# SSD convolutions in a queue of their own, and the last pair of an end stage leaving PSUM tile by tile

## The chip, the cores and the metric

The kernel runs on one core of one Trainium2 chip, in one launch. The metric is the device time of that core in microseconds. A core has five engines with a queue of instructions each: TensorE (PE in the profile, its weight loads PEld), VectorE (DVE), ScalarE (ACT), GpSimd (POOL) and SyncE (SP, which here issues most DMAs). Each works through its own queue in order, and waits at an instruction until what that needs from another engine is there.

## The reference

One step of a decoder layer for a prompt of 512 tokens and 8 sample requests of 4 tokens, which share the weights. All is fp32, D_MODEL is 1024.

```python
def layer(x, pos, rg_h0, rg_buf, ssd_h0, ssd_buf, p):
    x = x + 0.5 * rmsnorm(swiglu(rmsnorm(x, p['n_ffn1_pre']), p['ffn1_wg'], p['ffn1_wu'], p['ffn1_wd']), p['n_ffn1_post'])
    mix, new = mixer(rmsnorm(x, p['n_mix_pre']), pos, rg_h0, rg_buf, ssd_h0, ssd_buf, p)
    x = x + rmsnorm(mix, p['n_mix_post'])
    x = x + 0.5 * rmsnorm(swiglu(rmsnorm(x, p['n_ffn2_pre']), p['ffn2_wg'], p['ffn2_wu'], p['ffn2_wd']), p['n_ffn2_post'])
    return x, new
```

The mixer projects to one wide vector and works on two branches. The RG-LRU branch is a causal convolution over four tokens, two gates, a linear recurrence and a projection. The SSD branch is what the change touches:

```python
    xbc_c, ssd_buf_new = causal_conv(xbc, ssd_buf, p['ssd_conv_w'], p['ssd_conv_b'])
    xbc_c = jax.nn.silu(xbc_c.astype(f32))
    xs, Bs, Cs = jnp.split(xbc_c, [SSD_INNER, SSD_INNER + SSD_GROUPS * SSD_STATE], axis=-1)
    ...
    y, ssd_h_new = ssd_scan(xh, dt, A, Bs.reshape(b, l, SSD_GROUPS, SSD_STATE), Cs.reshape(b, l, SSD_GROUPS, SSD_STATE), ssd_h0)
    y = (y + p['ssd_d'][:, None] * xh).reshape(b, l, SSD_INNER) * jax.nn.silu(z.astype(f32))
```

There are 8 groups of 4 heads, with a state of 128 and chunks of 128 tokens; then come a grouped RMSNorm, a projection, a gated sum of the branches and an output projection. The last three inputs of each convolution are an output too (`ssd_buf_new`).

## The kernel before, in words

**Layout.** Prompt and samples are worked on together: 544 columns, in two halves of 272, with channels on the partitions. A matrix product is three products of rounded parts (high by high, low by high, high by low), so a block of 1024 by 128 weights takes 8 × 3 × 2 = 48 matmuls of 128x272. Such a block is a unit (`unit`, whose matmuls are L285): it fills one of two PSUM tiles named acc, of two banks each. `pair` takes one half of the columns and two blocks (L317 through `gemm_half`): bank j of acc is then tile j of the output. Weights come in blocks of 1 MB on SP's queue into wraw; ACT rounds a block to wh (L75) and DVE takes the rest as wl (L79), some blocks ahead of TensorE.

**Order.** TensorE's instructions run as they are written. The other engines' are put in order by a scheduler that goes by priorities; `urgent()` raises the priority of what stands under it. Small work for TensorE is woven between the matmuls of the units: `bg` is a list of generators, and after every `pace` matmuls (4 in the mixer, 5 after group 7's units) `ptick` calls `tick`, which runs the generator at the head up to its next `yield`. A generator starts when the one in front is through.

**The mixer.** After the RG-LRU pairs (`rg_steps`, four, of two tiles of 128 channels each) come eight SSD groups. For group g the units make four inputs of convolutions (B, C, and two tiles of x), then in some groups gates, then two tiles of z. For each of the four inputs ACT evacuates acc into a buffer cb (`conv_in`: L734 for the first half, L736 and L737 for the second) and copies the last three inputs of the prompt and of each sample to a small tile cq (`conv_last`, L877). Then a generator `conv_steps` is put behind in `bg`: it does the convolution (one ACT operation, L863, and three on DVE, L865), a tanh on ACT (L1009) and two products on DVE (L1010, L1011). In the second and the fourth of them, `conv_state` (from L879) first turns two cq tiles on TensorE (L884), copies them out on DVE (L887) and stores them. Behind these four, `bg` gets `group_steps`, which does the scan: A(c) for chunk c turns x and B into token order (L1041, L1043), evacuates them with DVE (L1056) and ACT (L1059) and makes the decays (L1048, L1062); Bs(c) makes the chunk's output (L1082, L1084) and state (L1086); s0, s1, s2 (L1165 with the evacuation L1168), s3 and s4 are for the samples; `fin` and the lines behind it finish the group. All tiles named ps share two PSUM buffers.

**End stages.** The last stage of FFN1, the output projection and FFN2 go through `y_units`, with halves and pairs. After a pair `evac_y` (L439 on DVE where the tile is added to what is there, or a copy on ACT), a square (L426), and a sum of squares (L433) follow. For the last pair (n2 == last) these are done tile by tile, but all of them after both tiles' matmuls. In FFN2's last pair, the final scaling yw (L1470) and turns to token order (L1474) follow at once.

## Time and profile before

| | |
|---|---|
| median of 3 runs | 1745.37 us (1741.66 to 1747.27) |
| the profiled execution's own time | 1746.04 us |
| its span, first to last instruction | 1744.2 us |
| TensorE busy | 1692.1 us, 97% |
| VectorE busy | 1000.7 us, 57% |
| ScalarE busy | 739.6 us, 42% |
| GpSimd busy | 260.4 us, 15% |
| mean granted clock of TensorE | 0.985 |

Times in the profile are microseconds from the start of the span. "L285" is line 285 of the kernel before. A row such as "PE ps L1041 <- ACT big L1168: 8.0, 5, 2.2" says that TensorE's instructions of line 1041 waited five times for ACT's of line 1168, for 8.0 us in all and 2.2 at most. In rows in order of time the first two numbers are start and length, and the bracket at the end gives the idle time of the engine just before, and who ended it. A PE row with x2 stands for two matmuls.

Groups 0 to 7 of the SSD branch lie between about 660 and 1075 us, FFN1 before 440 us, the output projection around 1240 to 1340 us and FFN2 behind it.

### The profile page before, as it was taken

The page shows a single profiled execution, that of the slowest core. Times are in us where ns is not written, and L with a number is a line of the kernel's source. Part 1 is how long each engine was busy: PE and PEld are TensorE (multiplying, and loading weights), DVE is VectorE, ACT ScalarE, POOL GpSimd, SP SyncE. Part 2 cuts the span into 40 slices and gives each one's busy share as a digit, 9 for nine tenths or more (in the row PEclk, how much of TensorE's full clock was granted, in tenths as well). Part 3 has the DMA queues.
Part 4 walks back from the last instruction along what each step waited for, and adds up shares of the span by engine and source line. Part 5 has one row for each costly group of instructions (what it writes and reads, how often), then busy time and mean ns, then how long its engine had stood idle before and what let it go on. Part 6 is the DMA issues. An engine that isn't in the chain of part 4 may idle for free. (4 is left out here: it accounts for less than half of the span.)

```text
span 1744.2 us, 32098 instructions
## 1 busy us (share of the span) xinstructions
PE 1692.1 (97%) x13485; PEld 1649.7 (95%) x13485; DVE 1000.7 (57%) x1764; ACT 739.6 (42%) x1204; POOL 260.4 (15%) x376
## 2 busy tenths in 40 slices
PE   8999999999999998999999999999999999999997
PEld 8899999999999997998988988999999999999997
DVE  5632333237757578788689687776558332233335
ACT  6323221234568674545545545434246423221233
POOL 0000000000222125345344333230000000000000
PEclk9999999999999998999999999999999999999999
DMA  6223232233543333524443535666324323223231
GB/s 208 84 75 114 74 98 84 87 97 109 164 156 112 101 97 107 165 88 113 146 144 93 157 114 155 214 189 221 137 80 139 115 68 109 85 85 97 75 120 52
DMA packets 205551, 206.21 MB, mean 118 GB/s; under 512 B 10461, under 2 KB 191785, under 8 KB 205150
## 3 DMA queue, kind: packets, MB, share of 16 engines
q1 hardware_dynamic: 196588, 178.49, 33.1%
q0 software_dynamic: 8336, 24.54, 4.3%
q8 instruction: 106, 1.74, 0.4%
q10 hardware_dynamic: 482, 1.12, 0.2%
q14 instruction: 39, 0.32, 0.1%
HBM read 178.43 MB, written 25.69 MB: 117 GB/s over the span
## 5 line engine op out<-in xcount | busy, mean ns | idle before, releaser
L75 ACT CAST wh<-wraw 128x1024 fp32r<-128x1024 f32 (+1 forms) x274 | 283.6, 1037 | 645.9 <-PE acc L285 535.0
L285 PE MATMUL acc<-xh,wh 128*128 128x272 f32 x2576 | 544.3, 292 | 0.1
L285 PE MATMUL acc<-xh,wl 128*128 128x272 f32 x2576 | 541.7, 292 | 0.0
L285 PE MATMUL acc<-xl,wh 128*128 128x272 f32 x2576 | 539.3, 291 | 0.0
L79 DVE TENSOR_TENSOR wl<-wraw,wh 128x1024 fp32r<-128x1024 f32 (+1 forms) x274 | 331.3, 1212 | 320.3 <-ACT wh L75 317.2
L285 PEld LDWEIGHTS acc<-xh,wh 128*128 128x128 f32 x2576 | 409.0, 190 | 3.5 <-issue 1.4
L285 PEld LDWEIGHTS acc<-xh,wl 128*128 128x128 f32 x2576 | 407.3, 190 | 2.6 <-issue 1.2
L285 PEld LDWEIGHTS acc<-xl,wh 128*128 128x128 f32 x2576 | 408.3, 190 | 1.2 <-issue 0.4
L317 PE MATMUL acc<-xh,wh 128*128 128x272 f32 x384 | 114.6, 298 | 3.3 <-DVE xl L571 3.3
L317 PE MATMUL acc<-xh,wl 128*128 128x272 f32 x384 | 113.8, 296 | 0.0
L317 PE MATMUL acc<-xl,wh 128*128 128x272 f32 x384 | 113.4, 295 | 0.0
L386 DVE TENSOR_TENSOR gate<-gate,acc 128x544 f32<-128x544 f32 x36 | 26.0, 721 | 132.0 <-PE acc L285 132.0
L865 DVE SCALAR_TENSOR_TENSOR cv<-cb,hp,cv 128x568 f32<-128x568 f32 x96 | 93.9, 978 | 1.1
L285 PE MATMUL acc<-hh,wh 128*128 128x272 f32 x448 | 92.5, 288 | 0.0
L285 PE MATMUL acc<-hl,wh 128*128 128x272 f32 x448 | 92.2, 287 | 0.0
L285 PE MATMUL acc<-hh,wl 128*128 128x272 f32 x448 | 92.2, 288 | 0.0
L1551 POOL TENSOR_TENSOR xtok<-xtok,yo 32x512 f32<-32x512 f32 x1 | 1.3, 1257 | 535.7 <-ACT yo L1550 535.7
L725 POOL MEMSET cb<- 128x3 f32 x40 | 4.1, 102 | 510.1 <-PE acc L317 434.7
L317 PEld LDWEIGHTS acc<-xh,wh 128*128 128x128 f32 x384 | 74.4, 194 | 3.9 <-DVE xl L571 3.4
L317 PE MATMUL acc<-hh,wh 128*128 128x272 f32 x256 | 75.0, 293 | 0.0
L317 PEld LDWEIGHTS acc<-xl,wh 128*128 128x128 f32 x384 | 74.4, 194 | 0.5
L317 PEld LDWEIGHTS acc<-xh,wl 128*128 128x128 f32 x384 | 74.2, 193 | 0.3
(397 smaller groups left out, 2642.5 us busy)
## 6 DMA issues: line engine op xcount, KB each, us to landing
wraw<-in_w_in_dram SPq DMA_DIRECT2D x34, 1024.0 KB, 5.6
wraw<-in_ffn_wu_dram SPq DMA_DIRECT2D x24, 1024.0 KB, 5.3
wraw<-in_ffn_wg_dram SPq DMA_DIRECT2D x23, 1024.0 KB, 5.2
wraw<-in_ffn_wd_dram SPq DMA_DIRECT2D x20, 1024.0 KB, 5.2
wraw<-in_w_in_dram SPq DMA_DIRECT2D x18, 512.0 KB, 4.3
big<-acs_dram SPq DMA_DIRECT2D x32, 256.0 KB, 5.6
big<-in_state_ssd_dram SPq DMA_DIRECT2D x32, 256.0 KB, 6.0
out_dram<-big POOLq DMA_DIRECT2D x32, 256.0 KB, 3.6
```

The costliest lines, as they stand in the source:

```text
L75: c = nc.scalar.copy(h[:, :kt], src)
L79: nc.vector.tensor_sub(l[:, :kt], src, h[:, :kt].bitcast(F32))
L285: PE.matmul(acc[:, h, :TH], w[:, k, :], r[k][:, HALF[h]], start=(k == 0 and i == 0), stop=(k == kt - 1 and i == 2))
L317: PE.matmul(acc[:, j, :TH], w[:, k, :], r[k][:, HALF[h]], start=(k == 0 and i == 0), stop=(k == kt - 1 and i == 2))
L386: V.tensor_mul(two(gs[j]), two(gs[j]), acc[:, :, :TH])
L725: G.memset(buf[:, 0:3], 0.0)
L865: V.scalar_tensor_tensor(o[:, :CO], buf[:, k:k + CO], ws[k], o[:, :CO], op0=ALU.mult, op1=ALU.add)
L1551: G.tensor_add(x[:n, cs], x[:n, cs], o[:n])
```

## The change

**First**, the four convolutions of a group are no longer generators in `bg`. They are plain functions (`conv_ssd`) in a list `convs`. `conv_next(g, limit)` takes the first of them if it is one of group g's, if fewer than `limit` of that group's have been taken, and if at least APART = 7 ticks have passed since the last. It is called at every `yield` of the group in front (`steps` in `group_steps`): the limit is 2 up to A(3), 3 up to s3(0) and Bs(2), 4 from there. The last RG-LRU pair takes up to two of group 0's. When `bg` is empty, `tick` takes one. What is left when a group starts is done at its start.

**Second**, `pair` takes a function `done(acc, j)`, called in program order after each tile's 24 matmuls. `y_units` gives it the evacuation for the last pair, so tile 0's evacuation, square, sum and (in FFN2) scaling are written ahead of tile 1's matmuls. Other pairs are as before.

```diff
+APART = 7
@@
+    def conv_take():
+        g, work = convs.pop(0)
+        work()
+        convs_done[g] += 1
+        conv_at[0] = ticks[0]
+
+    def conv_next(g, limit):
+
+        if convs and convs[0][0] == g and convs_done[g] < limit and ticks[0] >= conv_at[0] + APART:
+            conv_take()
+
     def tick():
+        ticks[0] += 1
         while bg:
...
+        if convs:
+            conv_next(convs[0][0], 4)
@@ pair
             gemm_half(acc, j, wbs[j], kt, rh, rl, h)
+            if done is not None:
+                done(acc, j)
@@ y_units
-            acc = pair(kt, rh, rl, h, keep if n2 in KEPT else None, n2)
...
-            step = 1 if n2 == last else 2
...
-            for j in range(0, 2, step):
+
+            def out(acc, j, step=1):
                 yv = yb[:, 2 * n2 + j:2 * n2 + j + step, HALF[h]]
                 with urgent():
                     evac_y(yv, acc[:, j:j + step, :TH], add)
...
+            acc = pair(kt, rh, rl, h, keep if n2 in KEPT else None, n2, out if n2 == last else None)
+            if n2 != last:
+                out(acc, 0, 2)
@@ rg_steps
+        def steps(n):
+            for _ in range(n):
+                yield
+                if r0 == KD - 2:
+                    conv_next(0, 2)
@@ conv_steps, now conv_ssd
-    def conv_steps(f, buf, res, i):
+    def conv_ssd(f, buf, res, i):
...
-        yield from wait(3)
@@ group_steps
+        while convs_done[g] < 4:
+            conv_take()
+            yield from wait(3)
         Bt, Ct, x0, x1, z0, z1 = (tiles[i] for i in range(6))
+        limit = [2]
+
+        def steps(n):
+            for _ in range(n):
+                yield
+                conv_next(g + 1, limit[0])
...
         A(3)
-        yield from wait(3)
+        limit[0] = 3
+        yield from steps(3)
         yield from s3(0)
         Bs(2)
-        yield from wait(3)
+        limit[0] = 4
+        yield from steps(3)
@@ the mixer's loop over groups
-            bg.append(conv_steps(f, buf, out, i))
+            convs.append((g, lambda f=f, buf=buf, out=out, i=i: conv_ssd(f, buf, out, i)))
```

Every other `wait` in `rg_steps` and `group_steps` is `steps` now. The lines of the change have other numbers: 285 is 307, 317 is 341, 439 is 466, 433 is 456, 734, 736 and 737 are 761, 763 and 764, 863 is 890, 865 is 892, 877 is 904, 884 is 911, 1009 is 1042, 1010 is 1043, 1041 and 1043 are 1083 and 1085, 1048 is 1090, 1059 is 1101, 1062 is 1104, 1082 to 1086 are 1124 to 1128, 1165 is 1207, 1168 is 1210, 1470 is 1514 and 1474 is 1518. Buffers are numbered differently too.

How the instructions stand now, at three places. The first is TensorE's queue in group 1, where a unit (acc_8030 in both) ends and the next begins; it is the second input of group 2's convolutions. Before:

```order
L285 MATMUL acc_8030<-xh7_102,wl_7702 128x272 x2
L285 MATMUL acc_8144<-xh0_95,wh_7802 128x272 x2
L285 MATMUL acc_8144<-xl0_103,wh_7802 128x272 x2
L1082 MATMUL py_8035<-big_7960,small_7969 64x128 [waits Pool_49]
...
L285 MATMUL acc_8646<-xh1_96,wh_8365 128x272 x2
L884 MATMUL ps_8656<-ident_71,cq_8022 27x128 [waits DVE_49]
L884 MATMUL ps_8656<-ident_71,cq_8138 27x128
```

And now:

```order
L307 MATMUL acc_8030<-xh7_102,wl_7756 128x272 x2
L307 MATMUL acc_8154<-xh0_95,wh_7819 128x272 x2
L307 MATMUL acc_8154<-xl0_103,wh_7819 128x272 x2
L911 MATMUL ps_8160<-ident_71,cq_8022 27x128 [waits Activation_49]
L911 MATMUL ps_8160<-ident_71,cq_8148 27x128 [waits Activation_49]
L1124 MATMUL py_8045<-big_7960,small_7969 64x128 [waits Pool_49]
```

The cq tile of the unit that has just ended (cq_8138 before, cq_8148 now) is read four matmuls into the next unit; before, it was read five units later. The row now waits for ACT.

The second place is ACT's queue at the same point. Before:

```order
L1168 COPY big_8103<-ps_8098 128x512
L1048 ACTIVATE big_8070<-big_8070 128x512
L1062 ACTIVATE big_7953<-big_7953 128x512
L1009 ACTIVATE cv_8624<-cv_8619 128x568
L75 CAST wh_8140<-wraw_7800 128x1024
L734 COPY cb_8132<-acc_8030 128x272
L736 COPY cb_8132<-acc_8030 128x240
L737 COPY cb_8132<-acc_8030 128x8x4
L877 COPY cq_8138<-cb_8132 128x27
L1168 COPY big_8122<-ps_8117 128x512
L863 ACTIVATE cv_8663<-cb_8132,hp_4848 128x568
```

And now:

```order
L1210 COPY big_8113<-ps_8108 128x512
L1042 ACTIVATE cv_8041<-cv_8036 128x568
L1090 ACTIVATE big_8080<-big_8080 128x512
L1104 ACTIVATE big_7953<-big_7953 128x512
L75 CAST wh_8150<-wraw_7817 128x1024
L761 COPY cb_8142<-acc_8030 128x272
L763 COPY cb_8142<-acc_8030 128x240
L764 COPY cb_8142<-acc_8030 128x8x4
L904 COPY cq_8148<-cb_8142 128x27
L890 ACTIVATE cv_8167<-cb_8142,hp_4848 128x568
L1210 COPY big_8132<-ps_8127 128x512
```

The copy to cq stands behind the same kinds of rows in both; the tanh (L1009, now L1042), of group 2's first convolution in both, comes two rows earlier, and the evacuation L1168 (now L1210) behind the copy has the next convolution's L863 (now L890) ahead of it instead of behind it.

The third place is the start of the last tile of FFN2 on TensorE (the second tile of the last pair), where hh and hl are the parts of the hidden activations. Before:

```order
L1474 MATMUL py<-ident,yw 128x128 [waits Activation_49]
L1474 MATMUL ps<-ident,yw 128x128 [waits PE_49]
L317 MATMUL acc<-hh,wh 128x272
L317 MATMUL acc<-hl,wh 128x272
L317 MATMUL acc<-hh,wl 128x272 [waits DVE_49]
```

And now:

```order
L1518 MATMUL py<-ident,yw 128x128 [waits Activation_49]
L1518 MATMUL ps<-ident,yw 128x128 [waits PE_49]
L341 MATMUL acc<-hh,wh 128x272 [waits DVE_49]
L341 MATMUL acc<-hl,wh 128x272
L341 MATMUL acc<-hh,wl 128x272
```

The tile's first matmul waits for DVE now, whose evacuation of the tile in front (L466) is written ahead of it.

## The prediction

> **What bounds the kernel now.** I read the page first, then the list of waits on TensorE for the mixer, then a table of stretches with the granted clock, then single stretches in order of time.

> ```profile
> span 1744.2 us, 32098 instructions
> ...
> PE 1692.1 (97%) x13485; PEld 1649.7 (95%) x13485; DVE 1000.7 (57%) x1764; ACT 739.6 (42%) x1204; POOL 260.4 (15%) x376
> ```

> TensorE sets the time: 1744.2 − 1692.1 leaves it 52 us without work, and the change neither adds nor removes a matmul of the units. So the time can move in three ways: a wait on PE goes, a wait on PE comes, or the clock that is granted changes. The waits of the mixer up to the output projection (560 to 1400 us; waited for: us in total, times, longest):

> ```profile
> PE ps L1041 <- ACT big L1168: 8.0, 5, 2.2
> PE ps L1043 <- DVE in L1010: 7.0, 2, 5.2
> PE ps L1165 <- ACT small L1059: 4.0, 3, 2.6
> PE ps L1041 <- DVE small L1144: 2.3, 4, 0.9
> ...
> PE ps L1132 <- ACT cq L877: 1.0, 1, 1.0
> ...
> PE ps L1086 <- ACT small L1059: 0.5, 2, 0.3
> ```

> These six are the SSD groups' own: 8.0 + 7.0 + 4.0 + 2.3 + 1.0 + 0.5 = 22.8 us. Stalls also cost clock. In the table of stretches the fields are the stretch, its length, the busy time and count of PE, PEld, DVE, ACT and POOL, the granted clock, the DMA share and GB/s:

> ```profile
> 640.00:680.00 40.00, 33.01 (x243) 31.99 (x242) 34.69 (x74) 22.92 (x44) 19.43 (x20) 0.87 0.50 148
> 720.00:760.00 40.00, 38.63 (x324) 36.82 (x323) 32.42 (x68) 21.07 (x41) 16.71 (x24) 1.00 0.43 123
> 800.00:840.00 40.00, 36.55 (x305) 33.36 (x304) 32.04 (x67) 18.19 (x41) 20.08 (x25) 0.96 0.33 94
> 920.00:960.00 40.00, 36.74 (x303) 34.52 (x301) 36.09 (x71) 19.38 (x42) 20.95 (x28) 0.96 0.32 90
> 1000.00:1040.00 40.00, 37.09 (x319) 33.89 (x319) 34.40 (x70) 15.74 (x33) 16.42 (x18) 0.96 0.38 118
> ```

> Four of the waits in order of time (start and length in us, and in brackets the idle time before and who ended it):

> ```profile
> 752.30 0.49 PE L1041 MATMUL ps<-in 128*128 128x128 f32 x2 [1.37 <-ACT big L1168]
> ...
> 820.50 0.49 PE L1041 MATMUL ps<-in 128*128 128x128 f32 x2 [1.95 <-ACT big L1168]
> ...
> 945.08 1.11 PE L1165 MATMUL ps<-ident,big 128*128 128x128 f32 x4 [2.58 <-ACT small L1059]
> ...
> 1014.99 0.49 PE L1041 MATMUL ps<-in 128*128 128x128 f32 x2 [2.22 <-ACT big L1168]
> ```

> The three stretches with one stall of 1.95, 2.58 and 2.22 us have 0.96; the stretch with 1.37 us has 1.00. At 0.96 a stretch of 40 us loses 0.04 × 40 = 1.6 us. The first stretch, with the 7.0 us of group 0, has 0.87: 0.13 × 40 = 5.2 us, of which part falls on the wait itself; I count 2.8. So clock adds 3 × 1.6 + 2.8 = 7.6, and the most that the first part of the change could give back is 22.8 + 7.6 = 30.4 us.

> **The change part by part. What goes.** A group's four convolutions stood in the one list of background steps, ahead of its steps; now they are taken between the steps of the group in front. The number of convolutions, their operations and their engines stay:

> ```profile
> L865 DVE SCALAR_TENSOR_TENSOR cv<-cb,hp,cv 128x568 f32<-128x568 f32 x96 | 93.9, 978 | 1.1
> L75 ACT CAST wh<-wraw 128x1024 fp32r<-128x1024 f32 x77 | 80.6, 1049 | 84.6 <-PE acc L285 84.4
> L863 ACT ACTIVATE cv<-cb,hp 128x568 f32<-128x568 f32 x32 | 27.6, 863 | 0.0
> L1009 ACT ACTIVATE cv<-cv 128x568 f32<-128x568 f32 x32 | 21.7, 677 | 50.7 <-DVE cv L865 50.6
> ```

> The big wait of group 0 (7.0, with its clock) stays for two thirds: two of its convolutions are still taken right ahead of its first step, and DVE is busy for 34.69 of 40 us there, so the same work in another order ends hardly earlier; I keep 4.6 of the 7.0 and 2 of the 2.8. Of the rest I let 2 us stay. 30.4 − 4.6 − 2 − 2 leaves **22 us off**.

> **What comes.** Two cq copies are turned by TensorE after each second convolution (before L884, after L911). Before, the order had them some hundred matmuls behind the unit that made the second copy. In the changed order (rows of both stand above) they come four matmuls after that unit's last one, and PE works in order: all that is queued behind L911, the next unit's matmuls among it, waits until ACT has made the copy (L877, after L904). What ACT does between a unit's end and that copy, on a busy and on a free ACT:

> ```profile
> 747.32 0.41 PE L285 MATMUL acc<-xh,wl 128*128 128x272 f32 x2
> 747.57 0.41 PE L285 MATMUL acc<-xh,wh 128*128 128x272 f32 x2
> ...
> 749.27 0.68 ACT L1009 ACTIVATE cv<-cv 128x568 f32<-128x568 f32 x1 [1.48 <-DVE cv L865]
> 749.85 1.03 ACT L75 CAST wh<-wraw 128x1024 fp32r<-128x1024 f32 x1
> 750.79 0.38 ACT L734 COPY cb<-acc 128x272 f32<-128x272 f32 x1
> 751.07 0.36 ACT L736 COPY cb<-acc 128x240 f32<-128x240 f32 x1
> 751.32 0.20 ACT L737 COPY cb<-acc 128x32 f32<-128x32 f32 x1
> 751.55 0.22 ACT L877 COPY cq<-cb 128x27 f32<-128x27 f32 x1
> ...
> 768.00 0.52 PE L285 MATMUL acc<-xh,wh 128*128 128x272 f32 x2
> ...
> 767.27 1.05 ACT L75 CAST wh<-wraw 128x1024 fp32r<-128x1024 f32 x1 [0.66 <-PE acc L285]
> 768.23 0.38 ACT L734 COPY cb<-acc 128x272 f32<-128x272 f32 x1
> ...
> 768.99 0.22 ACT L877 COPY cq<-cb 128x27 f32<-128x27 f32 x1
> ```

> The unit at 747.57 had just ended; four matmuls of the next take 0.5 us (two in 0.25 by the rows), so L911 would be asked for at 748.07 and have its copy at 751.77: 3.7 us. The unit at 768.00 would be asked at 768.5 and served at 769.21: 0.7 us. The order puts the copy behind the same rows on ACT as before: a tanh that waits for DVE's convolution, two exponentials, a weight cast, three evacuations.

> There are sixteen such places, two for each group's four convolutions. Seven are the first pairs of groups 1 to 7, taken while the group in front has its first steps' copies on ACT, as in the busy stretch: I take 3.5 each, a little under 3.7 as the tanh stands two rows further ahead now, 24.5. Eight others lie where ACT has less in front: between 0.7 and 1.9 (a weight cast more, 1.05 by its row), 1.1 each, 9. One stands eight matmuls behind and costs nothing. Together **33.5 us on**. Bounds: were ACT free everywhere, 15 × 0.7 = 10; as busy everywhere as at 747.57, 15 × 3.7 = 56. Below nothing it can't go, since the copy needs the unit.

> Seven stalls of 3.5 are longer than all three after which the clock dropped, so 7 × 1.6, **11 us on** (0 if no stall passes 1.4, as at 752.30).

> [...]

> **The second part.** The last pair of an end stage (FFN1, output projection, FFN2, each in both halves: six places) now leaves PSUM tile by tile in program order, so the first tile's evacuation may start while the second tile is multiplied. But in the changed order the second tile's first matmul waits for that evacuation (its row above says so), which it never did:

> ```profile
> 1729.83 1.52 PE acc L317 x12
> ...
> 1731.38 0.78 DVE yb L439 x2
> 1732.16 0.83 DVE yw L1470 x4
> ```

> At the end of the chain one of the two yb (0.78 / 2 = 0.39) and half of yw (0.42) are done earlier: 0.8 off; and the wait of 0.4 at the first half's end goes too. On the other side PE stops for the first tile's last matmul to end (0.29 of its row less 0.125 until the next starts), the evacuation of 0.39 and a handover, about 0.65, six times: 3.9; where a cast or the other half's closing work is in front on DVE, 1.2 at two of them, 1.1 more. 5.0 − 1.2 = **3.8 on** (between 1.2 off, if PE never had to wait, and 6 × 1.2 − 1.2 = 6 on).

> ```profile
> PE ps L459 <- DVE ld L433: 0.4, 1, 0.4
> ...
> 1729.80 0.29 PE L317 MATMUL acc<-hl,wh 128*128 128x272 f32 x1
> 1729.92 0.29 PE L317 MATMUL acc<-hh,wl 128*128 128x272 f32 x1
> ```

> The sum: −22 + 33.5 + 11 + 3.8 = +26. As stalls behind one another relieve each other (a PE that stands lets ACT catch up, so the next wait is shorter), I take off a fifth: +21. The profiled execution took 1746.04, 1.8 around its span of 1744.2, and lies 0.7 over the median of the three runs; so **1767 us**.

> **The rivals.**

> B, the other side: faster. ACT reaches the copy early, because the work that now jams it (the tanh of the group's own convolution, waiting 1.48 us for DVE at 749.27) has moved elsewhere; then the fifteen waits are 0.7 (10), or 1.3 (20), none costs clock, and the old stalls go. 1746 − 22 + 10 + 3.8 = 1738; with 20, 1748, no change; with all 30.4 gone and the 10, 1729. It decides at 1.2 us a wait: (22 − 3.8) / 15. For it speaks that ACT is busy for 21.07 of 40 us only; against it, that the order has the tanh in front of the copy again, and that PE asks at 0.5 us, sooner than the four copies (0.38 + 0.36 + 0.20 + 0.22, overlapping, 0.98 from 768.23) can be done.

> C, clock. The waits come as forecast, but the clock drops only after longer ones: −11, so 1755. The three rows with 0.96 speak against it.

> D, the change doesn't do what it says. The scheduler orders DVE and ACT by its own priorities, and already put a group's convolutions between the steps of the group in front (the tanh at 749.27 is one of group 2's, among group 1's copies). Then the old stalls stay, for the same work is as much in ACT's way, and the new ones come on top: 1767 + 22 = 1789; if neither moved, 1746. Against the first speaks that a wait at L911 lies just ahead of those at A(3): at 747.57 PE would stand for 3 us while ACT passes the very work that L1041 waits for 4.7 us later, at 752.30.

> **How the numbers follow.** The forecast, new waits larger than the old: 0.55, own range 1755 to 1785. B 0.27, of which 0.06 within 0.3%. C 0.08. D 0.10, of which 0.05 unchanged. For 8 in 10 the range has to take in the better part of B: 1735 to 1790. What a measurement here can tell from no change is 0.3%, 5 us: faster 0.21, same 0.11, slower 0.68.

> **What would show it.** In the waits on PE after the change: L911 waiting for ACT's cq (L904) some fifteen times, 25 to 40 us in all, the longest ones at 3 us and more; fewer than 12 us of it would be B. The waits L1041 on L1168 (after, L1083 on L1210) should be down from 8.0 to about 1. The granted clock should be 0.96 or less in 40 us stretches of groups 1 to 6, and 1.00 would be C or B. The wait of group 0 (after, L1085 on L1043) should still be 4 to 5 us. At the ends of the end stages L341 should wait for L466 or its ACT counterpart, 0.5 to 1.2 each. What makes the forecast wrong first is the size of the first pairs' waits: at 1.0 instead of 3.5 the sum is −22 + 16 + 0 + 3.8 = −2.2.

## The result, and the profile after

The changed kernel takes 1787.47 us (median of 4 runs, 1784.76 to 1788.94) against 1743.91 for the kernel before in the same comparison: 43.6 us more, a ratio of 1.0246 with a 95% interval of 1.0223 to 1.0270. The direction is the forecast one, and the time lies in the stated range of 1735 to 1790, near its upper end; it is over the 1755 to 1785 that the forecast gave for its own mechanism, and the loss is twice the 21 us that were forecast.

The page of the kernel after:

```profile
span 1787.1 us, 32121 instructions
...
PE 1705.4 (95%) x13485; PEld 1658.6 (93%) x13485; DVE 1003.4 (56%) x1764; ACT 743.1 (42%) x1205; POOL 264.4 (15%) x376
```

The span grew by 42.9 us. TensorE has the same 13485 instructions, but they took 13.3 us longer (1692.1 to 1705.4): that is clock, whose mean grant fell from 0.985 to 0.978. Its idle time grew from 52.1 to 81.7 us: 29.6 us of waits. The waits on TensorE in the kernel after, largest first (us in total, times, longest):

```profile
PE ps L911 <- ACT cq L904: 24.8, 14, 3.5
PE ps L1083 <- DVE small L1186: 4.8, 4, 1.3
PE ps L1085 <- DVE in L1043: 4.7, 1, 4.7
PE py L970 <- ACT in L972: 3.8, 2, 2.7
PE acc L307 <- DVE yb L1412: 3.1, 1, 3.1
PE acc L307 <- ACT th L1343: 3.1, 1, 3.1
...
PE ps L911 <- ACT small L1101: 2.6, 2, 1.3
PE acc L341 <- DVE yb L466: 2.5, 4, 1.0
PE ps L911 <- ACT cb L764: 2.4, 1, 2.4
...
PE ps L1207 <- DVE cs L914: 1.2, 1, 1.2
...
PE acc L353 <- ACT th L1376: 1.2, 1, 1.2
...
PE acc L341 <- ACT yb L468: 1.1, 2, 0.6
PE acc L1580 <- DVE acc L1575: 0.9, 1, 0.9
```

The new head of the list is L911, the transposes of the cq copies, which hardly waited before: 24.8 + 2.6 + 2.4 = 29.8 us in 17 waits. The waits of A(3) on L1168 (8.0 us before) and of s2 on L1059 (4.0) are gone from it; that of L1085 shrank from 7.0 to 4.7. The six rows of 22.8 us that the forecast set out from have 10.7 left (4.8, 4.7 and 1.2 of L1128 on L1101), and 1.8 came beside them (L1207 on L914 1.2, L1223 on L1210 0.6): 10.3 us were gained there. Three rows have no large counterpart before: L970 on L972 (3.8), and the projections' L307 on L1412 and on L1343 (3.1 each).

One of the waits at L911 in order of time, the place in group 1 that the forecast worked from. First TensorE, then ACT:

```profile
756.96 0.41 PE L307 MATMUL acc<-xl,wh 128*128 128x272 f32 x2
757.20 0.27 PE L911 MATMUL ps<-ident,cq 128*27 128x128 f32 x1
760.23 0.29 PE L911 MATMUL ps<-ident,cq 128*27 128x128 f32 x1 [2.75 <-ACT cq L904]
```

```profile
756.62 0.68 ACT L1042 ACTIVATE cv<-cv 128x568 f32<-128x568 f32 x1 [0.79 <-DVE cv L892]
757.21 0.63 ACT L1090 ACTIVATE big<-big 128x512 f32<-128x512 f32 x1
...
758.27 1.03 ACT L75 CAST wh<-wraw 128x1024 fp32r<-128x1024 f32 x1
759.20 0.38 ACT L761 COPY cb<-acc 128x272 f32<-128x272 f32 x1
...
759.96 0.22 ACT L904 COPY cq<-cb 128x27 f32<-128x27 f32 x1
```

The first of the two transposes runs at 757.20, the second stands until 760.23, and ACT is busy all the time with the very rows that the order showed: tanh, two exponentials, a cast, three evacuations, then the copy. 3.0 us between the two transposes, against 3.5 forecast for such a place.

### The profile page after: what moved, and what is told of

The parts are those of the page before. It is cut to its first block, busy times and chain, and to the rows that moved or that the text cites. A ratio compares the mean times of both kernels' runs of the same rounds, so it can differ in the third digit from the quotient of the medians.

```text
span 1787.1 us, 32121 instructions
## 1 busy us (share of the span) xinstructions
PE 1705.4 (95%) x13485; PEld 1658.6 (93%) x13485; DVE 1003.4 (56%) x1764; ACT 743.1 (42%) x1205; POOL 264.4 (15%) x376
## 5 line engine op out<-in xcount | busy, mean ns | idle before, releaser
L75 ACT CAST wh<-wraw 128x1024 fp32r<-128x1024 f32 (+1 forms) x274 | 283.8, 1037 | 663.2 <-PE acc L307 548.0
L307 PE MATMUL acc<-xh,wh 128*128 128x272 f32 x2576 | 546.9, 294 | 6.2 <-DVE yb L1412 3.1
L307 PE MATMUL acc<-xh,wl 128*128 128x272 f32 x2576 | 544.9, 293 | 0.0
L307 PE MATMUL acc<-xl,wh 128*128 128x272 f32 x2576 | 541.5, 292 | 0.0
L79 DVE TENSOR_TENSOR wl<-wraw,wh 128x1024 fp32r<-128x1024 f32 (+1 forms) x274 | 330.7, 1210 | 324.6 <-ACT wh L75 321.3
L307 PEld LDWEIGHTS acc<-xh,wh 128*128 128x128 f32 x2576 | 411.2, 191 | 10.1 <-issue 4.9
L307 PEld LDWEIGHTS acc<-xl,wh 128*128 128x128 f32 x2576 | 410.8, 191 | 2.3 <-issue 1.2
L307 PEld LDWEIGHTS acc<-xh,wl 128*128 128x128 f32 x2576 | 410.7, 192 | 1.6 <-issue 0.4
L341 PE MATMUL acc<-xh,wh 128*128 128x272 f32 x384 | 114.7, 299 | 3.0 <-DVE xl L598 3.0
L341 PE MATMUL acc<-xh,wl 128*128 128x272 f32 x384 | 114.0, 297 | 0.0
L341 PE MATMUL acc<-xl,wh 128*128 128x272 f32 x384 | 113.5, 296 | 0.0
L307 PE MATMUL acc<-hh,wh 128*128 128x272 f32 x448 | 92.5, 288 | 0.0
L307 PE MATMUL acc<-hl,wh 128*128 128x272 f32 x448 | 92.2, 287 | 0.0
L307 PE MATMUL acc<-hh,wl 128*128 128x272 f32 x448 | 92.1, 288 | 0.0
L892 DVE SCALAR_TENSOR_TENSOR cv<-cb,hp,cv 128x568 f32<-128x568 f32 x96 | 87.9, 916 | 0.7
L341 PEld LDWEIGHTS acc<-xh,wh 128*128 128x128 f32 x384 | 74.5, 194 | 3.6 <-DVE xl L598 3.1
L341 PE MATMUL acc<-hh,wh 128*128 128x272 f32 x256 | 75.3, 294 | 2.5 <-DVE yb L466 2.5
L341 PEld LDWEIGHTS acc<-xl,wh 128*128 128x128 f32 x384 | 74.6, 194 | 0.5
L341 PEld LDWEIGHTS acc<-xh,wl 128*128 128x128 f32 x384 | 74.3, 193 | 0.3
```

Of the source, the lines that this page charges most:

```text
L75: c = nc.scalar.copy(h[:, :kt], src)
L79: nc.vector.tensor_sub(l[:, :kt], src, h[:, :kt].bitcast(F32))
L307: PE.matmul(acc[:, h, :TH], w[:, k, :], r[k][:, HALF[h]], start=(k == 0 and i == 0), stop=(k == kt - 1 and i == 2))
L341: PE.matmul(acc[:, j, :TH], w[:, k, :], r[k][:, HALF[h]], start=(k == 0 and i == 0), stop=(k == kt - 1 and i == 2))
L892: V.scalar_tensor_tensor(o[:, :CO], buf[:, k:k + CO], ws[k], o[:, :CO], op0=ALU.mult, op1=ALU.add)
```

## The experiments

Each kernel was timed beside the kernel before; differences below are against that partner (1742.46, 1744.36, 1744.05 or 1743.24 us). The changed kernel stands at +43.6.

**The two parts apart.** First the queue of convolutions without the second part:

```diff
-            acc = pair(kt, rh, rl, h, keep if n2 in KEPT else None, n2, out if n2 == last else None)
-            if n2 != last:
-                out(acc, 0, 2)
+            acc = pair(kt, rh, rl, h, keep if n2 in KEPT else None, n2)
+            step = 1 if n2 == last else 2
+            for j in range(0, 2, step):
+                out(acc, j, step)
```

> The queue of convolutions alone; the last pairs leave PSUM after both tiles, as before. By the forecast's sum the second part costs 3.8 us, by the rows of the changed kernel 3.6 us of waits (L341 on L466 2.5, on L468 1.1) less 1.2 at the ends: so about 1784 to 1785, 2.5 to 4 under the changed kernel, and no wait of a second tile on the first one's evacuation. If the second part were neutral, 1787.

Measured: 1781.91 us, ratio 1.0225 (1.0210 to 1.0240), +39.5. L912 (L911 there) has the same three rows, 24.8, 2.6 and 2.4 us. So the first part makes nine tenths of the loss, and the second about 4.1 us of it (43.6 less 39.5).

Then the second part on the kernel before:

```diff
-    def pair(kt, rh, rl, h, keep=None, key=None):
+    def pair(kt, rh, rl, h, keep=None, key=None, done=None):
...
+            if done is not None:
+                done(acc, j)
```

with `y_units` as in the change.

> The second part alone, on the kernel before. If it costs what the forecast says, 2.5 to 4 us over the kernel before (1746 to 1748), with six waits of 0.4 to 1.2 us at the second tile of a last pair. If its early evacuation pays, it is level or up to 1 us faster.

Measured: 1746.83 us, ratio 1.0026 (1.0015 to 1.0036), +4.4; 39.5 + 4.4 is 43.9, so the two parts add up. Its waits on TensorE at the second tiles between 400 and 1450 us:

```profile
PE acc L319 <- DVE yb L444: 1.6, 2, 0.9
...
PE acc L319 <- ACT yb L446: 1.1, 2, 0.6
```

With two more on L444 at the end (0.9) these are the six, 3.6 us, 0.6 each. The chain of its end shows what was got for it:

```profile
1731.36 1.53 PE acc L319 x12
1732.91 0.45 DVE yb L444
1733.38 0.50 DVE yw L1475 x2
```

From the last matmul to the end of yw it takes 0.99 us, where it took 1.64 (1731.35 to 1732.99): 0.6 us back for 3.6 paid.

**Where the transposes stand.** In the changed kernel, the two transposes are issued eight ticks after their convolution is taken, and nothing else is moved:

```diff
+    states = []
+    def state_next(now=False):
+        while states and (now or ticks[0] >= states[0][0]):
+            states.pop(0)[1]()
...
     def tick():
         ticks[0] += 1
+        state_next()
...
-            conv_state(o_p_ssd_conv, o_s_ssd_conv, [lasts.pop(0) for _ in range(2)], f - df, df)
+            qs = [lasts.pop(0) for _ in range(2)]
+            states.append((ticks[0] + 8, lambda: conv_state(o_p_ssd_conv, o_s_ssd_conv, qs, f - df, df)))
```

> The changed kernel, but the two transposes of the cq copies are issued eight ticks (32 matmuls, 4 us) after their convolution is taken instead of with it. Theory A (TensorE stands because the transposes come four matmuls after the unit): the longest wait, 3.5 us, is covered; the waits at the transposes fall from 29.8 us to under 3, and the half-clock stretches behind them (15 us of clock lost in all) go; up to 8 + 4 us of the old waits at A(3) and s2 come back. 1787 - 28 - 13 + 8 = 1750 to 1758. Theory B (ScalarE and VectorE are crowded by convolutions that come earlier, and the wait shows wherever TensorE next asks for them): the waits move to the groups' own steps, and the time stays above 1775.

Measured: 1762.25 us, ratio 1.0111 (1.0096 to 1.0126), +19.8: 24 us of the loss are gone. No wait at the transposes on the cq copy is left. TensorE's busy time is 1698.4 us, 7.0 less than in the kernel after: clock. The waits in the mixer now:

```profile
PE py L976 <- ACT in L978: 4.9, 2, 2.7
PE ps L1214 <- issue: 4.1, 1, 4.1
PE ps L1230 <- ACT small L1108: 3.9, 2, 2.1
...
PE acc L313 <- DVE yb L1419: 3.1, 1, 3.1
PE acc L313 <- ACT th L1350: 2.8, 1, 2.8
...
PE ps L917 <- DVE small L1142: 0.9, 2, 0.4
```

L917 is the transposes: 0.9 us. So the place on TensorE made the waits (theory A). But the time is 4 to 12 us over what A expected. The clock gave back 7.0 us where A had 13. Of the old waits A had let 8 us come back; 4.1 came at s2 (L1214; "issue" says that the profile shows nothing it waited for) and 1.5 at A (L1090 on L1217). L1230 (3.9, and 1.1 more on L1217) is a wait in the groups' own steps that the kernel before did not have and the changed one with 0.6 only; those at L976 and L313 the changed kernel had already. A part of theory B is true: the other engines are still late, and TensorE meets some of it elsewhere.

The same with two ticks instead of eight:

> The changed kernel with the transposes two ticks (8 matmuls, 1.0 us) later instead of eight. If the place on TensorE alone sets the waits, each of the eleven long ones shrinks by 1.0 us and the five of 0.4 go: 29.8 to about 17 to 19 us in all, and two or three half-clock stretches of 1.7 us with them: 1770 to 1775. If ScalarE and VectorE simply fall behind by as much, the waits stay at 25 to 30 and the time over 1783.

Measured: 1768.05 us, ratio 1.0139 (1.0122 to 1.0156), +23.7. The waits at the transposes:

```profile
PE ps L917 <- ACT cq L910: 8.3, 5, 3.6
PE ps L917 <- DVE small L1140: 5.3, 1, 5.3
...
PE ps L917 <- ACT big L1217: 1.5, 3, 0.8
...
PE ps L917 <- ACT small L1108: 0.6, 2, 0.3
```

15.7 us where 29.8 were, and 0.9 with eight ticks. The waits shrank a little more than 1.0 us a place would give (17 to 19 were expected to be left), and 5.3 of what is left is a single wait of another kind, for a PSUM buffer that DVE sets free. With 1.0 us of distance most of what 4 us of distance gave back is given back (19.9 of 23.8).

**The last RG-LRU pair.** The changed kernel without group 0's two early convolutions:

```diff
     def steps(n):
         for _ in range(n):
             yield
-            if r0 == KD - 2:
-                conv_next(0, 2)
```

> The changed kernel without the two convolutions of group 0 in the last RG-LRU pair. The tanh among that pair's sigmoids brings a table load of 1.28 us each way and 3.8 us of waits at L970 on L972, which the forecast did not have, and a wait of 0.8 at a transpose: these 4.6 us and one half-clock stretch (1.7) go; the wait of group 0's first step grows from 4.7 towards the 7.0 of before, with 1.7 of clock. Net 1784 to 1787. If the table loads are hidden, nothing changes in the waits at L970.

Measured: 1781.31 us, ratio 1.0221 (1.0206 to 1.0237), +38.9, so 4.7 us under the changed kernel, more than expected. The wait of 3.8 us at L970 on L972 is gone. ACT in the kernel after, where it arises:

```profile
626.82 1.28 ACT L1042 ACT_TABLE_LOAD   x1 [5.65 <-DVE cv L892]
...
628.80 1.28 ACT L972 ACT_TABLE_LOAD   x1
630.10 0.73 ACT L972 ACTIVATE in<-py,pT 128x568 f32<-128x568 f32 x1
```

ACT stands for 5.65 us until DVE's convolution is there for the tanh, and the sigmoid behind it, for which TensorE's next gate waits, stands with it. The sigmoid's input is ready at 624.79, where TensorE's L970 ends, and it runs at 630.10. Of these 5.3 us some 2.0 are the wait for the tanh's input, 2.56 the two table loads and 0.7 the tanh itself: the queue and the tables share the cost. In the kernel without the two, group 0's first step waits 5.6 us instead of 4.7, so taking them early had given it 0.9 us.

**The last group.** The changed kernel, with group 7's convolutions at its own start:

```diff
             yield
-            conv_next(g + 1, limit[0])
+            if g < 6:
+                conv_next(g + 1, limit[0])
```

> The changed kernel, but group 7's four convolutions are not taken between group 6's steps; they stand at group 7's start as before. Theory: the two waits of 3.1 us at the first projections (L307 on L1343 and on L1412), which the forecast did not have, come because group 7 runs ahead and holds the six buffers that the projection's loads need; then they fall to the 0 and 1.5 of before, with 3.4 us of clock; group 7's own waits at its transposes (4.8 and 1.4, with 3.4 of clock) go too. About 1770. If those two waits have another cause, they stay and only group 7's own go: about 1778.

Measured: 1774.95 us, ratio 1.0172 (1.0156 to 1.0187), +30.6, so 13 us under the changed kernel, between the two expectations. The waits at the transposes fell from 29.8 to 23.8 (20.1 + 2.4 + 1.3); that on L1412 went (0.6 is left, at L353), that on L1343 fell from 3.1 to 1.6 only. The wait on L1412 is 3.1 in p1_alone, no_rg, late8 and late2 too, where group 7 is early, so its going is the edit's doing. That on L1343 is 1.6 in p1_alone and 1.3 in no_rg as well, with group 7 as early as before, so its fall here says nothing of group 7. In the kernel after ACT stands behind a load there:

```profile
1138.75 0.65 ACT L249 CAST xh<-in 128x544 fp32r<-128x544 f32 x1 [3.16 <-DMA in<-yr_dram]
...
1140.41 0.63 ACT L1343 ACTIVATE th<-acc 128x544 f32<-128x544 f32 x1
...
1141.09 0.52 PE L307 MATMUL acc<-xh,wh 128*128 128x272 f32 x2 [3.06 <-ACT th L1343]
```

A cast waits 3.16 us for the projection's input, the evacuation L1343 stands behind it, and a unit waits for acc. The loads go into the tiles named `in`, of which there are six, and a group's convolutions take four. That group 7's early start holds them is argued from this; the run shows only that the wait on L1412 goes with it. The wait behind the load is taken up again by the last run below.

**All of it taken back but the queue.** Late transposes, no early convolutions in the RG-LRU pair, last pairs as before:

> Three edits together: transposes eight ticks later, no convolution in the last RG-LRU pair, and last pairs as before. By the single runs: 1762 less 6 (no_rg against the changed kernel) less 5 (the two readings of the second part, 4.4 and 5.6): 1751, 9 us slower than the kernel before. If the terms overlap, 1755.

Measured: 1755.59 us, ratio 1.0061 (1.0046 to 1.0076), +11.2. Against their partners the single edits sum to 19.8 − 4.7 − 4.1 = 11.0 us, so they add up. The 9 of the expectation came from times that had been measured beside different partners.

With group 7 at its own start besides:

> The same with group 7 as before too. If the waits at the projections come from group 7's early start, 1751 less 4.5 of waits and 3.4 of clock: about 1743, level with the kernel before or up to 3 us faster, since the old waits at A(3) (8.0) come back only in part (1.5 in late8). If not, 1751.

Measured: 1748.33 us, ratio 1.0020 (1.0011 to 1.0029), +4.0. It lies between the two expectations: 7.2 us came back with group 7, and a wait of 3.0 at the projections (L1350) stayed. So the queue without these side effects does not pay either, at this point. Its largest waits in the mixer:

```profile
PE ps L1092 <- DVE in L1049: 5.5, 2, 5.2
PE ps L1214 <- issue: 4.1, 1, 4.1
PE ps L1090 <- DVE small L1193: 3.8, 3, 1.5
PE acc L313 <- ACT th L1350: 3.0, 1, 3.0
```

Two runs asked what the 4.1 is. In order of time it ends at 805.00, 0.11 us after DVE's L1140 has emptied a ps buffer (804.49, 0.40 long). More distance between the convolutions:

```diff
-APART = 7
+APART = 16
```

> The kernel of late8_p1_no_rg_g7 with APART = 16 ticks for 7, so that a group's second and fourth convolutions come 16 to 76 matmuls later. Its longest wait in the groups, 4.1 us at s2's transposes in group 3, ended when VectorE, which had two convolutions' last products and a slowed decay step in front, set a PSUM buffer free. If the closeness of the two convolutions makes that queue, the 4.1 us and the half-clock stretch behind it (1.7) go: about 1742 to 1744, level with the kernel before or a little faster. If VectorE has as much in front wherever they stand, 1747 to 1750.

Measured: 1746.21 us, ratio 1.0018 (1.0009 to 1.0027), +2.2. The row of 4.1 is gone, and waits of 1.7 to 1.9 came at other places (L1230 on L1217, L1090 on L771 and on L921), so only 1.8 us of 5.8 were got, and 1.8 is not clear of the noise: each of the two intervals reaches 1.6 us to either side. With one convolution instead of two before A(3):

```diff
-        limit = [2]
+        limit = [1]
```

> The kernel of late8_p1_no_rg_g7 with only one convolution (instead of two) taken before A(3) of the group in front. The same question asked by number instead of distance: if fewer convolutions among the group's first steps take VectorE's queue away, the 4.1 us at s2 go and the time is 1742 to 1745; the second convolution then stands behind A(3), among s3's work, and if VectorE is as late there, 1747 to 1752.

Measured: 1751.16 us, ratio 1.0050 (1.0033 to 1.0066), +7.1. The 4.1 stays, and L1237 waits 5.3 us more for DVE's L1242 (five waits): by its place the second convolution is in the way there. A smaller number does harm, and what distance gives is not clear.

Last, the kernel with APART = 16, and group 7 beginning 46 ticks later:

```diff
+        if g == 7:
+            yield from wait(46)
         while convs_done[g] < 4:
             conv_take()
```

> The kernel of all_apart16, but group 7 begins 46 ticks (184 matmuls, 23 us) later, about where it stood before the change; nothing else moves. Its largest wait that the kernel before does not have is 3.0 us of a projection unit on the gate's tanh (L1350), behind casts that wait for the projection's loads, with 1.7 us of clock. If it comes from group 7 running ahead of those loads, both go: 1746 less 4.7, so about 1741 to 1742, 2 to 3 us faster than the kernel before. If it comes from something else, the time stays at 1745 to 1747.

Measured: 1743.09 us against 1743.24, ratio 0.9998 (0.9989 to 1.0007). The wait of 3.0 us fell to 0.7, and no cast waits for a load of yr_dram there any more (1.27 and 0.83 us with APART = 16 alone): it did come from group 7 running ahead of the projection's loads. The time fell by 2.4 us against the partners where 4.7 were expected, and is level with the kernel before, not 2 to 3 us under it. The queue of convolutions, with most of what it brought along taken away (the transposes, L918, still wait 3.7 us), is worth nothing that can be measured, and no run beat the kernel before.

## Why the prediction was right or wrong

**What bounds the kernel, and the mechanism: right; the size: half.** The loss is waits and clock on TensorE, the largest wait is L911 on the copy of the unit that has just ended, and moving the transposes alone takes 24 of the 43.6 us away. What the sum had wrong is the clock (8 us too little), two places that it did not have (9 us), the old waits (6 us too much taken off) and the fifth that it took off at the end (5 us); L911 itself came out 4 us under its term.

**"33.5 us on": 29.8 measured.** The seven first pairs, forecast as 24.5, took 2.90, 2.75, 2.44 + 0.74, 3.48, 1.29 + 3.53, 2.75 and 1.29 + 3.48 us, 24.6 in all. The lighter places took 5.1 (0.76, four times 0.39, and 1.40 twice) where 9 were forecast. Rival B decided at 1.2 us a wait over fifteen places; 29.8 over fifteen is 2.0.

**"22 us off": too much.** Of the 22, some 16 were waits and the rest clock. 10.3 us of waits went. The rows that the forecast watched did go, L1168's and L1059's, 12 us; but A's wait on the samples' small tile grew from 2.3 to 4.8, and two smaller ones came. In late8_p1_no_rg_g7, where the transposes no longer stand in front, the rows of A (L1090) have 3.8 and 1.5 us (8.0 and 2.3 before), those of s2 (L1214) 4.1 and 1.2 (4.0 before), and L1230, which had none before, 2.4 and 1.1: 14.1 us in the place of 14.3. So the old waits moved and hardly shrank. The likely reason, which no run isolates, is that ACT and DVE have the same work, as rival D argued from the order, and that what they are late with shows at another row.

**Clock, "11 us on" less the 5.6 that the old stalls had cost: 5.4 net forecast, 13.3 measured.** The forecast let a stall cost 1.6 us. Three stretches of the kernel after, in the fields of the prediction's table:

```profile
680.00:720.00 40.00, 36.71 (x306) 33.70 (x306) 30.91 (x63) 15.35 (x32) 18.93 (x27) 0.91 0.24 65
...
920.00:960.00 40.00, 33.38 (x256) 31.70 (x254) 33.35 (x67) 20.65 (x39) 14.30 (x23) 0.91 0.40 115
...
1200.00:1240.00 40.00, 36.89 (x274) 36.70 (x274) 20.95 (x27) 11.44 (x14) 1.13 (x2) 0.91 0.52 159
```

Each has 0.91: 0.09 × 40 = 3.6 us, twice the 1.6. They hold the waits of 2.90, of 1.29 and 3.53, and of 3.11 us. The last one is at the projections, where the forecast had no stall. Read in stretches of 0.2 us, the clock between 620 and 1240 us is at half for fifteen times 3.41 us in the kernel after and for seven times in the kernel before: eight more, at 1.7 us each (half of 3.41), are 13.6. Nine of the fifteen stand behind first pairs, where seven had been forecast, and two at the projections. One of the seven first pairs (2.75 us, ending at 1025.08) cost no clock, and its stretch from 1000 to 1040 us stands at 1.00, where the forecast had asked for 0.96 or less.

**Taking off "a fifth": wrong.** Stalls were to relieve each other. The first pairs, forecast without any relief, measured 24.6 us for 24.5, so none shows there, and taking the fifth off moved the forecast 5 us away from the result.

**What the forecast did not have:** the last RG-LRU pair (3.8 us of waits, 4.7 in the experiment with its clock) and the first projections (3.1 + 3.1 + 1.2 where 1.9 stood, 5.5). Both stand in the change itself: the call in `rg_steps` puts a tanh that waits for DVE among the sigmoids of the RG-LRU pair, and the groups' earlier start moves group 7 into the time of the projection's loads. The forecast looked at the rows around L911 and not at what else a convolution issues, or holds.

**The second part, "3.8 on": right.** 4.4 measured (2.6 to 6.3 by the interval). By rows both of its sides are smaller than forecast: 3.6 us of waits for 5.0, and 0.6 back at the end and 0.4 at L459 for 1.2. The rest of the 4.4 is not found in rows.

The waits and the clock together: 29.8 − 10.3 + 3.8 + 5.5 + 3.0 (second part by its rows) + 13.3 = 45.1, for 42.9 of span; the 2 us between are waits at L477 and its like that are shorter in the profiled execution after.

The rivals: B falls, and so does C as far as it had the loss without the clock: TensorE's busy time grew by 13.3 us. D is true in half: what ACT and DVE do did not get out of the way. Its 1789 is the forecast nearest to the measured 1787, but by luck: it had all the old waits stay, and 10.3 us of them went, while more clock and two places that no rival had made up for it. That the result still fell into the stated range is in part luck too, since the range was drawn wide downwards for B and only 5 us above the forecast's own.

## What to carry to other kernels

When work is moved earlier in an engine's queue, list every instruction that it issues, and for each what it reads, when that is ready, and what stands behind it: here a convolution could well go early, but two small transposes inside it cost 30 us of waits, because they read copies of what TensorE had finished half a microsecond before, and ACT makes those copies behind other work. Delaying only those by 8 matmuls gave back five sixths of what delaying them by 32 did. A wait that disappears from its row is not gained as long as the engine that was late has as much work in front; here it showed at the next rows (14.1 us for 14.3).

## What the runs showed of the hardware that was not expected

In these runs the granted clock does not follow from the length of a stall alone. In the kernel after two stalls of exactly the same length, 2.75 us, end at 760.23 and at 1025.08. Stretches during and behind each (fields as in the prediction's table; the clock is the third from the end):

```profile
757.00:760.20 3.20, 0.48 (x4) 0.19 (x3) 2.95 (x4) 3.17 (x9) 1.33 (x2) 1.00 0.00 0
760.80:764.20 3.40, 3.40 (x21) 2.89 (x18) 2.17 (x5) 0.73 (x2) 1.54 (x3) 0.51 0.61 162
1022.00:1025.00 3.00, 0.32 (x3) 0.03 (x1) 2.75 (x4) 2.97 (x9) 1.27 (x1) 1.00 0.00 0
1025.00:1030.00 5.00, 4.92 (x44) 4.49 (x44) 4.71 (x11) 1.81 (x4) 3.49 (x4) 1.00 0.40 110
```

Behind the first the clock is at half for 3.4 us (0.51), behind the second at full. In two kernels that are alike up to that place, all_apart16 and the one with group 7's wait, stalls of nearly one length differ as well: a stall of 1.94 us that ends at 798.34 and one of 1.95 that ends at 801.27. Of the first kernel:

```profile
798.34 0.46 PE L1090 MATMUL ps<-in 128*128 128x128 f32 x2 [1.94 <-ACT cb L771]
...
800.00:804.00 4.00, 3.06 (x27) 2.84 (x25) 3.97 (x10) 0.83 (x3) 3.17 (x4) 1.00 0.00 0
```

And of the second:

```profile
801.27 0.74 PE L1092 MATMUL ps<-in 128*128 128x128 f32 x2 [1.95 <-ACT cb L771]
...
800.00:804.00 4.00, 2.73 (x12) 2.76 (x13) 3.94 (x6) 2.99 (x9) 4.00 (x3) 0.66 0.02 5
```

Behind the first the clock stays at full; behind the second it is at half for 3.4 us, 0.66 in the mean of this stretch.

So length alone does not decide here: behind a stall of 1.95 us the clock went to half in one kernel, and behind one of 2.75 us in another it did not.

The stalls of 1.94 and 1.95 us are no case of sharing: in the pieces of their own kernels each lies nearly whole in one, busy for 1.56 us in all_apart16 and 1.46 in the kernel with group 7's wait, so idle for 0.54 and 0.57. In all_apart16 the first, idle for 0.54, was not followed by half clock, and another piece, idle for 0.49, was. So no share of idle time separates the two outcomes in all of these traces, and what sets the clock was not shown. Of these two stalls, equal in length to 0.01 us, one cost a stretch at half clock, an estimated 1.7 us (half of 3.41), and the other nothing.
